# Latent attention with a new opening, split projections and rotations in steps

## The chip, the cores and the metric

The kernel runs on one core of a Trainium2 chip. The metric is the device time of one execution in microseconds (us); smaller is better. The core's engines each work through a queue of their own, in its order: TensorE (PE; its weight loads are shown as PEld), VectorE (DVE), ScalarE (ACT), GpSimd (POOL) and SyncE (SP), which issues most DMAs; ACT's queue issues some. An instruction whose input is not there holds up everything behind it on its engine.

## The reference

Three transformer layers run on 512 positions of width 1024. Only the first layer's mixer and one vector of the last layer matter here. The first mixer is a latent attention with 16 heads:

```python
h = x @ w_in                                   # 512 (c_q) + 256 (c_kv) + 32 (k_rope) columns
q  = (rms_norm(c_q, q_norm) @ w_uq)            # per head 64 plain columns + 32 to rotate
kv = (rms_norm(c_kv, kv_norm) @ w_ukv)         # per head 64 key columns + 64 value columns
q = [q_nope, apply_rope(q_rope)];  k = [k_nope, apply_rope(k_rope)]   # k_rope shared by all heads
out = causal softmax(q k^T / sqrt(96)) @ v;    return out @ w_o
```

In the last layer, `c_act = silu(c)` (1024 numbers) is multiplied with a large matrix to give shifts and scales. All inputs are float32.

## The kernel before

**Precision.** Each operand of a product is split into a high part, rounded by a cast, and a low part, the rest. A product is three matmuls (`mm3`): high by high, and twice high by low. So each weight block ("unit") is loaded as `raw` by SP, cast to `wh` on ACT (L121), and subtracted to `wl` on `lo_eng` (L122): DVE, but POOL inside the attention loop. Activations are split the same way by `split` (ACT cast L160, DVE subtract L161). PE's three matmuls are lines L153 to L155.

**Units.** `use()` hands out the next unit and first prepares all units up to `ahead` further ones (`ensure`, `_prep`), and loads `dma_ahead` beyond. Units 0 to 7 are `w_in`, 8 and 9 the query rotation weights, 10 the values of heads 0 to 7 ("v"), 11 the keys of heads 0 to 7 ("k"), 12 the queries of four heads ("q0"), 13 the values of heads 8 to 15 ("v1"), 14 the next queries ("q1"), 15 further keys ("k1"), 16 and 17 further queries. From 18 on come units of the cross-attention, used as fillers (`FILL_A`).

**Opening.** `front` transposes tiles of 128 positions of x (`tr`, L509) and multiplies them with `w_in`: tiles 0 and 1 together, then 2, then 3. `norm` forms the squared sums on ACT, a chain of small DVE steps (L537 to L184) for the reciprocal root, and `cn` (L542). `back` transposes `cn` (L553) and splits it into `cq` and `ckv`. `trig` makes cosines and sines. Then come the rotated query parts `rq`, in two halves of 256 positions; the second half needs tile 3.

**Attention.** In turn h the kernel runs: the output of head h-3 (`o`), the transposes of head h-2 (`t`, split to `pt`), the normalisation of head h-1 (DVE RECIPROCAL L700, then four products on POOL, L703), the scores of head h (`s`, L689; a DVE pass with the mask L692, then four exponentials on ACT L694), the routine `ahead(h)`, and fillers. `ahead(h)` of an even h projects keys (6 matmuls) and queries (12 matmuls) of the next pair of heads (`proj`, `qk`), and in turns 0, 4 and 8 runs a rotation (`rope`: a DVE shuffle L385, two products L386 and L387, a sum L388, a split) of four heads' queries. `FILL_V` says in which turns blocks of the value projection of heads 8 to 15 run: {1: (0,), 3: (1,), 4: (2, 3)}.

**Order.** The code is not the order. A scheduler of the framework moves each engine's instructions forward as its own model of the time allows; what stands in an engine's queue is fixed at build time. Loads leave SP in the order written: x tiles 0 and 1 with the eight `w_in` units, then eight small tables (`setup`), then x tiles 2 and 3, then the units for q, k and v. The vector `c` is loaded by ACT's queue at the start (`cc`) and used some 400 us later, in `mod_start`, by one ACTIVATE (`cact`, L1003).

Of the kernel before, what the change touches and what calls it, by code (L numbers as in the profile page):

```python
# [9 lines left out]
F = mybir.dt.float32  # L10
# [4 lines left out]
OP = mybir.AluOpType  # L15
# [17 lines left out]

FILL_A = {8: 1, 10: 2, 11: 2, 12: 1, 15: 1, 16: 2, 17: 3}
FILL_B = {2: 1, 3: 1, 4: 1, 6: 1, 9: 1, 11: 1, 12: 1, 14: 1, 17: 1, 19: 1, 20: 1, 22: 1, 24: 1, 27: 1, 28: 1}
FILL_V = {1: (0,), 3: (1,), 4: (2, 3)}
FILL_P = {7: (0,), 8: (1,), 9: (2,), 10: (3,)}
C_ID = 0
C_MASK = 128
# [25 lines left out]
class K:  # L65
# [311 lines left out]
        v.tensor_scalar(cos, cos, -2.0, 1.0, op0=OP.mult, op1=OP.add)  # L377
        self.cos, self.sin = cos, sin

    def rope(self, src, out, eng):  # L380

        nc = self.nc
        t = self.pg(F, "rp")
        t1, t2 = t[:, 0:512], t[:, 512:1024]
        nc.vector.stream_shuffle(t2, src, [(i + 16) % 32 for i in range(32)])  # L385
        eng.tensor_tensor(t1, src, self.cos, op=OP.mult)  # L386
        eng.tensor_tensor(t2, t2, self.sin, op=OP.mult)  # L387
        nc.vector.tensor_tensor(t1, t1, t2, op=OP.add)  # L388
        self.split(out[:, 0], out[:, 1], t1)
# [92 lines left out]
    def mla(self):  # L482
        nc, a = self.nc, self.a
        xd = a["x"][0].rearrange("(t p) d -> p t d", p=128)
        xs = []
        for t in range(NT):
            x = self.pg(F, "x0")
            if t == 0:
                nc.scalar.dma_start(x[:, 512:1024], xd[:, t, 512:1024])
                nc.sync.dma_start(x[:, 0:512], xd[:, t, 0:512])  # L490
            else:
                last = nc.sync.dma_start(x, xd[:, t, :])
            xs.append(x)
            self.load(1 if t == 0 else 8)
            if t == 1:
                self.setup(last)
        us = []
        cq = [[self.pg(R, "cq").rearrange("p (f c) -> p f c", f=2) for _ in range(2)] for _ in range(2)]
        ckv = [self.pg(R, "ckv").rearrange("p (f c) -> p f c", f=2) for _ in range(2)]
        cqs = [[cq[k // 2][h][:, k % 2] for h in range(2)] for k in range(4)]  # L500
        ckvs = [[ckv[h][:, k] for h in range(2)] for k in range(2)]
        krf = self.pg(F, "krf")[:, 0:512]

        def tr(t):
            xT = [self.pg(R, "x0T").rearrange("p (f c) -> p f c", f=8) for _ in range(2)]
# [9 lines left out]
        x0T = {}  # L515

        def front(ts, then=None):
            xT = [x0T.pop(t) if t in x0T else tr(t) for t in ts]
            pp = [(self.ps("pa"), self.ps("pb")) for _ in ts]
            for k in range(8):  # L520
                if len(us) == k:
                    us.append(self.use(3))
                u = us[k]
                for x, (pa, pb) in zip(xT, pp):
                    l = [x[0][:, k], x[1][:, k]]
                    self.mm3(pa, l, [u[0][:, 0:512], u[1][:, 0:512]], k == 0, k == 7)
                    self.mm3(pb[:, 0:288], l, [u[0][:, 512:800], u[1][:, 512:800]], k == 0, k == 7)
                if k == 4 and then is not None:
# [20 lines left out]
        def back(t, scr):  # L549
            c = slice(t * 128, t * 128 + 128)  # L550
            p = self.ps("tp")
            for f in range(4):
                nc.tensor.transpose(p[:, f * 128:(f + 1) * 128], scr[:, f * 128:(f + 1) * 128], self.ident)  # L553
            q = self.ps("tp")
            for f in range(3):
                nc.tensor.transpose(q[:, f * 128:(f + 1) * 128], scr[:, 512 + f * 128:512 + (f + 1) * 128], self.ident)
            p = p.rearrange("p (f c) -> p f c", f=4)
            for i in range(2):
                self.split(cq[i][0][:, :, c], cq[i][1][:, :, c], p[:, 2 * i:2 * i + 2])
            self.split(ckv[0][:, :, c], ckv[1][:, :, c], q[:, 0:256].rearrange("p (f c) -> p f c", f=2))  # L560
            nc.scalar.copy(krf[:, t * 128:(t + 1) * 128], q[:, 256:384])
# [6 lines left out]
        scr.append(norm(2, *pp[2]))  # L568
        self.trig()
        pp += front((3,))  # L570
        back(2, scr[2])
        prev = norm(3, *pp[3])
        self.ahead, self.dma_ahead = 2, 2
        QF = [[self.pair("qf") for _ in range(2)] for _ in range(2)]
        KF = [[self.pair("kf") for _ in range(2)] for _ in range(2)]
        for i in range(2):
            nc.gpsimd.memset(QF[i][1][0:32].bitcast(F), 0.0)
            nc.gpsimd.memset(KF[i][1][0:32].bitcast(F), 0.0)
        ropeq, rps = [], []
        uu = [self.use(), self.use()]  # L580
        for m in range(4):
            rps.append(self.ps("rq"))
        for g in range(2):
            if g == 1:
                back(3, prev)
            for m in range(4):
                for k in range(4):
                    cc = (m % 2) * 128
                    self.mm3(rps[m][:, g * 256:(g + 1) * 256],
                             [uu[m // 2][0][:, k, cc:cc + 128], uu[m // 2][1][:, k, cc:cc + 128]],  # L590
                             [x[:, g * 256:(g + 1) * 256] for x in cqs[k]], k == 0, k == 3)
            if g == 0:
                st = {n: self.use() for n in ("v", "k", "q")}
        V = {}

        def vproj(h, js=range(NT)):
            if h == 1 and js[0] == 0:
                st["v"] = self.use()
            u = st["v"]
            for j in js:  # L600
                p = self.ps("v")
                c = slice(j * 128, j * 128 + 128)
                for k in range(2):
                    self.mm3(p, [x[:, c] for x in ckvs[k]], [u[0][:, k], u[1][:, k]], k == 0, k == 1)
                V[h, j] = self.pair("v")
                self.split(V[h, j][:, 0], V[h, j][:, 1], p)

        kr = self.pair("kr")
        self.rope(krf, kr, nc.vector)
        rsb = [self.pg(F, "rsb") for _ in range(2)]  # L610
        rsb = [rsb[m // 2][:, (m % 2) * 512:(m % 2) * 512 + 512] for m in range(4)]

        def ropes(m):
            rq = self.pair("rq")
            self.rope(rsb[m], rq, nc.vector if m == 0 else nc.gpsimd)
            ropeq.append(rq)
        nc.scalar.copy(rsb[0], rps[0])
        ropes(0)
        for m in range(1, 4):
            nc.scalar.copy(rsb[m], rps[m])  # L620
        for i in range(2):
            nc.scalar.dma_start(KF[i][0][64:96].bitcast(F), kr[64:96].bitcast(F))
            nc.scalar.dma_start(KF[i][1][32:64].bitcast(F), kr[32:64].bitcast(F))
        OT = []
        vproj(0)

        def proj(p):
            if p == 4:
                st["k"] = self.use()
            if p in (2, 4, 6):  # L630
                st["q"] = self.use()
            ring = p % 2
            for hd in range(2):
                h = 2 * p + hd
                rows = slice(64, 96) if hd == 0 else slice(32, 64)
                nc.scalar.dma_start(QF[ring][hd][rows].bitcast(F), ropeq[h // 4][32 * (h % 4):32 * (h % 4) + 32].bitcast(F))
            for src, nk, w, cc, dst in ((ckvs, 2, st["k"], (p % 4) * 128, KF), (cqs, 4, st["q"], (p % 2) * 128, QF)):
# [360 lines left out]
    def mod_start(self):  # L998
        nc, a, cp = self.nc, self.a, self.cp
        cc = cp.tile([128, 8], F, name="cc")  # L1000
        nc.scalar.dma_start(cc, a["c_2"].rearrange("o (k p) -> p (o k)", p=128))
        self.cact = cp.tile([128, 8], F, name="cact")
        self.after(nc.scalar.activation(self.cact, cc, AF.Silu), self.last_act)  # L1003
        self.onesr = cp.tile([128, 128], R, name="onesr")
        nc.vector.tensor_copy(self.onesr, self.ones1.to_broadcast([128, 128]))
        self.modcol = cp.tile([128, 6, 8], F, name="modcol")
        self.gate = {}
        self.mstep, self.mw, self.macc, self.mlimit, self.mpend = 0, {}, {}, 16, None
# [694 lines left out]
```

## Time and profile before

| | us |
|---|---|
| three runs | 2175.51, 2175.67, 2180.46 (median 2175.67) |
| profiled execution, its own time | 2170.42 |
| its span, first to last instruction | 2168.6 |
| PE busy | 2125.2 (98%) |
| DVE / ACT / POOL busy | 1324.1 / 925.7 / 287.9 |
| mean granted TensorE clock | 0.995 of full |

Busy shares alone say that PE bounds the kernel. The changed code covers the first 245 us (the latent attention up to its output projection) and one place near 410 us.

### The profile page before, as it was taken

The page shows a single profiled execution, that of the slowest core. Times are in us where ns is not written, and L with a number is a line of the kernel's source. Part 1 is how long each engine was busy: PE and PEld are TensorE (multiplying, and loading weights), DVE is VectorE, ACT ScalarE, POOL GpSimd, SP SyncE. Part 2 cuts the span into 40 slices and gives each one's busy share as a digit, 9 for nine tenths or more (in the row PEclk, how much of TensorE's full clock was granted, in tenths as well). Part 3 has the DMA queues.
Part 4 walks back from the last instruction along what each step waited for, and adds up shares of the span by engine and source line. Part 5 has one row for each costly group of instructions (what it writes and reads, how often), then busy time and mean ns, then how long its engine had stood idle before and what let it go on. Part 6 is the DMA issues. An engine that isn't in the chain of part 4 may idle for free.

```text
span 2168.6 us, 30013 instructions
## 1 busy us (share of the span) xinstructions
PE 2125.2 (98%) x11492; PEld 1776.7 (82%) x11492; DVE 1324.1 (61%) x2747; ACT 925.7 (43%) x1684; POOL 287.9 (13%) x288
## 2 busy tenths in 40 slices
PE   8999999999999999899999999999999999999998
PEld 7789898988888887775688888888888879888886
DVE  6776566735237267877676845446377677755734
ACT  3687444313225143578734332224224655343521
POOL 0255100000000002476300000000004310000002
PEclk9999999999999999999999999999999999999999
DMA  6123613355324132240332345444320335432311
GB/s 209 49 67 99 205 59 117 96 167 155 97 94 151 54 107 65 77 123 27 125 119 79 117 155 184 136 127 159 104 59 21 88 112 156 146 94 91 126 59 39
DMA packets 254178, 233.82 MB, mean 108 GB/s; under 512 B 14516, under 2 KB 219700, under 8 KB 254036
## 3 DMA queue, kind: packets, MB, share of 16 engines
q1 hardware_dynamic: 246384, 214.19, 32.1%
q10 hardware_dynamic: 7652, 17.73, 2.6%
q8 instruction: 90, 1.47, 0.3%
q14 instruction: 52, 0.43, 0.1%
HBM read 220.81 MB, written 6.82 MB: 105 GB/s over the span
## 4 chain that ended last, share of the span: by engine, by line
PE 53%; DVE 4%; ACT 2%; issue 1%; POOL 0%; DMA 0%; DVEq 0%; ACTq 0%; POOLq 0%
PE fm L154 9%; PE fm L155 9%; PE fm L153 9%; PE acc L153 6%; PE acc L154 6%; PE acc L155 6%; PE s L1252 1%; PE o L153 1%; PE o L154 1%; PE o L155 1%; DVE sc L1172 1%; PE t L1275 1%; PE v L153 1%; DVE qb L1222 1%; DVE m L1169 1%
## 5 line engine op out<-in xcount | busy, mean ns | idle before, releaser
L154 PE MATMUL fm<-xT,wh 128*128 128x512 f32 (+3 forms) x1640 | 588.8, 361 | 0.4
L155 PE MATMUL fm<-xT,wl 128*128 128x512 f32 (+3 forms) x1640 | 588.3, 359 | 0.0
L153 PE MATMUL fm<-xT,wh 128*128 128x512 f32 (+3 forms) x1640 | 587.7, 360 | 0.5 <-ACT wh L121 0.4
L122 DVE TENSOR_TENSOR wl<-raw,wh 128x1024 fp32r<-128x1024 f32 (+1 forms) x299 | 358.3, 1223 | 94.5 <-ACT wh L121 64.4
L121 ACT CAST wh<-raw 128x1024 fp32r<-128x1024 f32 (+2 forms) x339 | 338.9, 1038 | 71.8 <-PE acc L154 18.8
L154 PEld LDWEIGHTS fm<-xT,wh 128*128 128x128 f32 (+2 forms) x1640 | 307.2, 187 | 48.4 <-DVE xT L250 1.6
L155 PEld LDWEIGHTS fm<-xT,wl 128*128 128x128 f32 (+2 forms) x1640 | 307.4, 187 | 47.2 <-DVE wl L122 0.3
L153 PEld LDWEIGHTS fm<-xT,wh 128*128 128x128 f32 (+2 forms) x1640 | 306.4, 187 | 48.2 <-ACT wh L121 0.9
L122 POOL TENSOR_TENSOR wl<-raw,wh 128x1024 fp32r<-128x1024 f32 (+1 forms) x40 | 93.4, 2344 | 1211.3 <-ACT wh L121 610.6
L153 PE MATMUL acc<-wh,hs 128*128 128x512 f32 x528 | 205.6, 389 | 0.0
L154 PE MATMUL acc<-wl,hs 128*128 128x512 f32 x528 | 205.4, 389 | 0.0
L155 PE MATMUL acc<-wh,hs 128*128 128x512 f32 x528 | 204.9, 389 | 0.0
L974 DVE TENSOR_TENSOR hT<-sil,fm 128x512 f32<-128x512 f32 x44 | 30.3, 688 | 228.5 <-PE fm L155 225.7
L973 ACT ACTIVATE sil<-fm 128x512 f32<-128x512 f32 x44 | 26.3, 598 | 300.6 <-PE fm L155 283.5
L153 PEld LDWEIGHTS acc<-wh,hs 128*128 128x128 f32 x528 | 99.1, 188 | 20.5
L957 DVE SCALAR_TENSOR_TENSOR cv<-fm,cw,cv 128x511 f32<-128x511 f32 x88 | 65.8, 748 | 82.2 <-ACT cv L955 81.0
L154 PEld LDWEIGHTS acc<-wl,hs 128*128 128x128 f32 x528 | 99.1, 188 | 20.5
L155 PEld LDWEIGHTS acc<-wh,hs 128*128 128x128 f32 x528 | 99.1, 188 | 20.5
L153 PE MATMUL acc<-wh,ot 128*128 128x512 f32 x288 | 112.5, 391 | 0.0
L155 PE MATMUL acc<-wh,ot 128*128 128x512 f32 x288 | 112.1, 389 | 0.0
L154 PE MATMUL acc<-wl,ot 128*128 128x512 f32 x288 | 112.1, 389 | 0.0
L217 ACT ACTIVATE x<-x,mv 128x1024 f32<-128x1024 f32 x20 | 24.9, 1243 | 147.9 <-DVE mv L216 147.8
(363 smaller groups left out, 3518.7 us busy)
## 6 DMA issues: line engine op xcount, KB each, us to landing
raw<-in_ffn_w_in_dram SPq DMA_DIRECT2D x88, 512.0 KB
mw<-in_mod_w_dram SPq DMA_DIRECT2D x48, 512.0 KB
raw<-in_ffn_w_down_dram SPq DMA_DIRECT2D x44, 512.0 KB
raw<-in_ffn_up_dram SPq DMA_DIRECT2D x44, 512.0 KB
raw<-in_xa_w_kv_dram SPq DMA_DIRECT2D x32, 512.0 KB
raw<-in_ffn_down_dram SPq DMA_DIRECT2D x22, 512.0 KB
raw<-in_xa_w_q_dram SPq DMA_DIRECT2D x16, 512.0 KB
raw<-in_xa_w_o_dram SPq DMA_DIRECT2D x16, 512.0 KB
```

Of the source, the lines that this page charges most:

```text
L121: self.nc.scalar.copy(hi[:, :n], raw[:, :n])
L122: self.lo_eng.tensor_tensor(lo[:, :n], raw[:, :n], hi[:, :n].bitcast(F), op=OP.subtract)
L153: mm(out, l[0], r[0], start=first, stop=False, **kw)
L154: mm(out, l[0], r[1], start=False, stop=False, **kw)
L155: mm(out, l[1], r[0], start=False, stop=last, **kw)
L217: ops.append(lambda: nc.scalar.activation(x, x, AF.Identity, bias=mv[:, 3:4], scale=mv[:, 2:3]))
L957: nc.vector.scalar_tensor_tensor(y[:, sh:], p[:, :S - sh], w[:, 2 - sh, c:c + 1], y[:, sh:], op0=OP.mult, op1=OP.add)
L973: nc.scalar.activation(s, g, AF.Silu)
L974: nc.vector.tensor_tensor(hT[j // 2][:, j % 2], s, u, op=OP.mult)
L1169: m = v.max(m8, sc[b])
L1172: v.match_replace(sc[b], m8, sc[b], -3.0e38)
L1222: ops.append(lambda o=o, i=i: v.tensor_copy(o, i))
```

## The change

- **Loads.** x tiles 2 and 3 are issued before the small tables of `setup`.
- **Front.** The first weight unit is taken after the first tile's transposes, ahead of the second's; the first four products run as block 0 and 1 of tile 0, then of tile 1.
- **Units.** `ahead` is 0 with `dma_ahead` 2 for the units 8 to 13, all taken before or just after the norm of tile 3; then `ahead` is 2. Unit 13 is taken there too. After it nothing is prepared further until q1 is taken, inside turn 3; q1, k1 and q2 are then prepared at once.
- **Values.** Two blocks of v (12 matmuls) run ahead of `back(3)`, two blocks of v1 after `proj(0)`; `FILL_V` keeps the other two.
- **Rotations** are cut into steps. That of the shared key and the first of the queries run interleaved on DVE; the later three follow the table `ROPE` (turn: which rotation, how many steps). The key rows of the first pair are copied sooner, those of the second pair after `proj(0)`.
- **Projections** of a pair: keys in the even turn, queries in the odd one.
- **c** is loaded by ACT's queue after `last_act`, the ACTIVATE `x` (L217) of the last tile, just ahead of its use.

No instruction kind is added or dropped; one `wl` subtraction goes from DVE to POOL.

```diff
-FILL_V = {1: (0,), 3: (1,), 4: (2, 3)}
+FILL_V = {3: (2,), 4: (3,)}
+ROPE = {0: ((1, 2),), 1: ((1, 2),), 3: ((2, 2),), 4: ((2, 1),), 5: ((2, 1),), 7: ((3, 2),), 8: ((3, 1),), 9: ((3, 1),)}
...
-            if t == 1:
-                self.setup(last)
+        self.setup(last)
...
-            xT = [x0T.pop(t) if t in x0T else tr(t) for t in ts]
+            xT = []
+            for t in ts:
+                xT.append(x0T.pop(t) if t in x0T else tr(t))
+                if not us:
+                    us.append(self.use(0))
...
+            if len(ts) == 2:
+                order[:4] = [(0, 0), (1, 0), (0, 1), (1, 1)]
...
+        self.ahead, self.dma_ahead = 0, 2
+        uu = [self.use(), self.use()]
+        st = {"v": self.use()}
         back(2, scr[2])
         prev = norm(3, *pp[3])
-        self.ahead, self.dma_ahead = 2, 2
+        for n in ("k", "q", "v1"):
+            st[n] = self.use()
+        self.ahead = 2
...
             if g == 1:
+                vproj(0, (0, 1))
                 back(3, prev)
...
-            if g == 0:
-                st = {n: self.use() for n in ("v", "k", "q")}
...
+        ks, qs = self.rope_steps(krf, kr, nc.vector), self.rope_steps(rsb[0], ropeq[0], nc.vector)
+        for x, n in ((ks, 1), (qs, 1), (ks, 2), (qs, 1), (ks, 1), (qs, 2)):
+            for _ in range(n):
+                x.pop(0)()
+        krows(0)
...
-        vproj(0)
+        vproj(0, (2, 3))
...
-            if h in (0, 4, 8):
-                ropes(h // 4 + 1)
-            if h % 2 == 0 and h < 14:
-                proj(h // 2 + 1)
+            for m, n in ROPE.get(h, ()):
+                ropes(m, n)
+            if h < 14:
+                proj(h // 2 + 1, (h % 2,))
         proj(0)
+        krows(1)
+        vproj(1, (0, 1))
...
-        nc.scalar.dma_start(cc, a["c_2"].rearrange("o (k p) -> p (o k)", p=128))
+        self.after(nc.scalar.dma_start(cc, a["c_2"].rearrange("o (k p) -> p (o k)", p=128)), self.last_act)
```

PE's queue from the scores of head 3 on, before (`s` scores, `v` value projection, `qk` key or query projection; the numbers tell buffers apart):

```order
L689 MATMUL s_1080<-kf_596,qf_592 128x512 x3
L689 MATMUL s_1078<-kf_596,qf_592 128x384 x3
L689 MATMUL s_1078<-kf_596,qf_592 128x128 x3
L689 MATMUL s_1079<-kf_596,qf_592 128x256 x3
L153 MATMUL v_1104<-wh_663,ckv_114 128x512
L154 MATMUL v_1104<-wl_664,ckv_114 128x512
```

and in the changed kernel:

```order
L713 MATMUL s_1055<-kf_612,qf_608 128x512 x3
L713 MATMUL s_1053<-kf_612,qf_608 128x384 x3
L713 MATMUL s_1053<-kf_612,qf_608 128x128 x3
L713 MATMUL s_1054<-kf_612,qf_608 128x256 x3
L155 MATMUL qk_1102<-cq_110,wh_1084 128x512
L156 MATMUL qk_1102<-cq_111,wh_1084 128x512
L157 MATMUL qk_1102<-cq_110,wl_1085 128x512
```

Behind the scores of head 3 there were value matmuls; now there are the query matmuls with the unit q1 (`wh_1084`, `wl_1085`).

POOL's queue in the same turn, before (`P`, `p` probabilities of a head, `rp` a rotation):

```order
L703 TENSOR_TENSOR P_1081<-P_1081,st_1083 128x512
L703 TENSOR_TENSOR P_1081<-P_1081,st_1083 128x384
L703 TENSOR_TENSOR P_1081<-P_1081,st_1083 128x128
L703 TENSOR_TENSOR p_1082<-p_1082,st_1083 128x256
L386 TENSOR_TENSOR rp_1183<-rsb_748,trig_487 128x512
L387 TENSOR_TENSOR rp_1183<-rp_1183,trig_487 128x512
L703 TENSOR_TENSOR P_1159<-P_1159,st_1161 128x512
```

and in the changed kernel, where `P_1056` and `p_1057` are head 3's:

```order
L389 TENSOR_TENSOR rp_1080<-rsb_755,trig_487 128x512
L390 TENSOR_TENSOR rp_1080<-rp_1080,trig_487 128x512
L727 TENSOR_TENSOR P_1056<-P_1056,st_1058 128x512
L727 TENSOR_TENSOR P_1056<-P_1056,st_1058 128x384
L727 TENSOR_TENSOR P_1056<-P_1056,st_1058 128x128
L124 TENSOR_TENSOR wl_1085<-raw_597,wh_1084 128x1024
L727 TENSOR_TENSOR p_1057<-p_1057,st_1058 128x256
L124 TENSOR_TENSOR wl_1091<-raw_603,wh_1090 128x1024
L124 TENSOR_TENSOR wl_1097<-raw_1088,wh_1096 128x1024
```

Three subtractions of weights (q1, k1, q2) now follow head 3's normalisation; `wl_1085`, the first, stands behind three of its four products.

DVE's queue in the same turn of the changed kernel (`st_1058` is head 3's sums; ISA is the pass with the mask):

```order
L716 ISA p_1057,st_1058<-s_1054,cst 128x256
L716 ISA st_1058 128x1
L391 STREAM_SHUFFLE rp_1080<-rsb_755 128x512
L392 TENSOR_TENSOR rp_1080<-rp_1080 128x512
L724 RECIPROCAL st_1058<-st_1058 128x4
L163 TENSOR_TENSOR qf_605<-qk_1102,qf_605 64x512
L163 TENSOR_TENSOR qf_606<-qk_1102,qf_606 64x512
```

A shuffle and a sum of the rotation, which takes POOL's `rp_1080` products, stand ahead of head 3's reciprocal.

DVE's queue in the norm of tile 3, before (`rs`, `ss` its small steps):

```order
L182 TENSOR_TENSOR rs_572<-ss_568 128x2
L183 TENSOR_TENSOR rs_572<-rs_572 128x2
L184 SCALAR_TENSOR_TENSOR ss_568<-rs_572,ss_568 128x2
L542 SCALAR_TENSOR_TENSOR cn_567<-pa_501,ss_568,nrows_95 128x512
L543 SCALAR_TENSOR_TENSOR cn_567<-pb_502,ss_568,nrows_95 128x256
L545 COPY cn_567<-pb_502 128x128
L122 TENSOR_TENSOR wl_602<-raw_271,wh_601 128x1024
L161 TENSOR_TENSOR cq_111<-tp_675,cq_110 128x2x128
L122 TENSOR_TENSOR wl_658<-raw_289,wh_657 128x1024
```

and in the changed kernel:

```order
L184 TENSOR_TENSOR rs_572<-ss_568 128x2
L185 TENSOR_TENSOR rs_572<-rs_572 128x2
L124 TENSOR_TENSOR wl_590<-raw_271,wh_589 128x1024
L186 SCALAR_TENSOR_TENSOR ss_568<-rs_572,ss_568 128x2
L124 TENSOR_TENSOR wl_594<-raw_289,wh_593 128x1024
L184 TENSOR_TENSOR rs_572<-ss_568 128x2
L124 TENSOR_TENSOR wl_600<-raw_307,wh_599 128x1024
L185 TENSOR_TENSOR rs_572<-rs_572 128x2
L186 SCALAR_TENSOR_TENSOR ss_568<-rs_572,ss_568 128x2
L184 TENSOR_TENSOR rs_572<-ss_568 128x2
```

The subtractions of the units k, q0 and v1, which followed `cn`, now stand between the small steps ahead of it.

## Rows read from the trace of the kernel before

**Rows 1.** By stretch: us, busy per engine (instructions), PEclk, DMA share, GB/s

```profile
0.00:45.00 45.00, 37.85 (x202) 32.71 (x203) 24.78 (x61) 19.62 (x37) 4.29 (x9) 1.00 0.66 216
45.00:81.00 36.00, 31.39 (x191) 28.02 (x189) 29.38 (x72) 16.29 (x36) 1.29 (x1) 0.95 0.28 84
81.00:131.00 50.00, 49.11 (x273) 41.38 (x274) 39.86 (x108) 39.22 (x94) 26.45 (x30) 0.97 0.21 54
```

**Rows 2.** Waits of PE, 0 to 245 us; awaited work, us in total, times, longest

```profile
PE tp L553 <- DVE cn L542: 3.0, 1, 3.0
PE o L153 <- ACT pt L160: 1.7, 2, 1.3
PE s L689 <- ACT qf L160: 1.7, 1, 1.7
...
PE o L154 <- DVE pt L161: 1.1, 2, 0.6
```

**Rows 3.** Waits of the SP queue, 0 to 30 us; same columns

```profile
SPq L113 <- DMA cc<-in_c_dram: 6.9, 1, 6.9
```

**Rows 4.** Timeline of PE, opening; start, us, operation, [idle before <- releaser]

```profile
7.42 1.97 PE L509 MATMUL tp<-cst,x 128*128 128x128 f32 x8 [0.19 <-DMA x<-in_x_dram]
10.83 0.79 PE L153 MATMUL pa<-wh,x0T 128*128 128x512 f32 x1 [1.43 <-ACT wh L121]
...
24.34 1.07 PE L509 MATMUL tp<-cst,x 128*128 128x128 f32 x8 [0.53 <-DMA x<-in_x_dram]
```

**Rows 5.** Timeline of ACT, opening

```profile
9.91 5.42 ACT L121 CAST wh<-raw 128x800 fp32r<-128x800 f32 x7
```

**Rows 6.** Timeline of DVE, norm of tile 3

```profile
57.74 0.16 DVE L537 TENSOR_TENSOR ss<-ss,cst 128x2 f32<-128x2 f32 x1
...
60.31 0.75 DVE L542 SCALAR_TENSOR_TENSOR cn<-pa,ss,nrows 128x512 f32<-128x512 f32 x1
...
61.57 1.22 DVE L122 TENSOR_TENSOR wl<-raw,wh 128x1024 fp32r<-128x1024 f32 x1
```

**Rows 7.** Timeline of PE, v projection

```profile
71.98 0.39 PE L155 MATMUL v<-wh,ckv 128*128 128x512 f32 x1
...
74.70 0.39 PE L155 MATMUL v<-wh,ckv 128*128 128x512 f32 x1
```

**Rows 8.** Clock after the wait for tile 3; columns of rows 1

```profile
63.00:66.00 3.00, 3.00 (x12) 2.61 (x11) 2.90 (x5) 1.68 (x4) 0.00 (x0) 0.50 0.00 0
```

**Rows 9.** Timeline of PE, scores of heads 0 and 4

```profile
81.55 2.80 PE L689 MATMUL s<-kf,qf 96*128 96x512 f32 x11 [0.21 <-DVE kf L161]
...
108.74 2.16 PE L689 MATMUL s<-kf,qf 96*128 96x512 f32 x12
```

**Rows 10.** Timeline of DVE, heads 2 and 4

```profile
97.78 0.68 DVE L692 CUSTOM_DVE_ANT_0 P<-s,cst 128x512 f32<-128x512 f32 x1
...
100.83 0.18 DVE L700 RECIPROCAL st<-st 128x4 f32<-128x4 f32 x1 [1.33 <-ACT p L694]
...
112.94 0.68 DVE L692 CUSTOM_DVE_ANT_0 P<-s,cst 128x512 f32<-128x512 f32 x1
...
116.73 0.69 DVE L388 TENSOR_TENSOR rp<-rp 128x512 f32<-128x512 f32 x1 [0.85 <-POOL rp L387]
```

**Rows 11.** Timeline of POOL, heads 0 to 4

```profile
92.00 0.61 POOL L703 TENSOR_TENSOR p<-p,st 128x256 f32<-128x256 f32 x1
...
98.07 2.41 POOL L122 TENSOR_TENSOR wl<-raw,wh 128x1024 fp32r<-128x1024 f32 x1
...
109.75 2.19 POOL L703 TENSOR_TENSOR P<-P,st 128x512 f32<-128x512 f32 x3 [5.84 <-PE s L689]
```

**Rows 12.** Timeline of ACT, after the output projection

```profile
412.07 0.21 ACT L1003 ACTIVATE cact<-cc 128x8 f32<-128x8 f32 x1
...
416.58 1.24 ACT L217 ACTIVATE x<-x,mv 128x1024 f32<-128x1024 f32 x1 [2.41 <-DVE mv L216]
```

**Rows 13.** Timeline of PE there

```profile
420.78 1.91 PE L232 MATMUL tp<-cst,x 128*128 128x128 f32 x16
```

More of the change, by code (lines that the diff above doesn't have):

```diff
@@ L378, in trig, with rope_steps @@
         self.cos, self.sin = cos, sin
-    def rope(self, src, out, eng):
+    def rope_steps(self, src, out, eng):
         nc = self.nc
@@ L384, in rope, with products @@
         t1, t2 = t[:, 0:512], t[:, 512:1024]
[L385 to L389, printed above, removed]
+        def products():
+            eng.tensor_tensor(t1, src, self.cos, op=OP.mult)
+            eng.tensor_tensor(t2, t2, self.sin, op=OP.mult)
+        return [lambda: nc.vector.stream_shuffle(t2, src, [(i + 16) % 32 for i in range(32)]), products,
+                lambda: nc.vector.tensor_tensor(t1, t1, t2, op=OP.add), lambda: self.split(out[:, 0], out[:, 1], t1)]
     def plan(self):
@@ L517, in front @@
         def front(ts, then=None):
-            xT = [x0T.pop(t) if t in x0T else tr(t) for t in ts]
+            xT = []
[3 more added lines that the diff above has]
+                    us.append(self.use(0))
             pp = [(self.ps("pa"), self.ps("pb")) for _ in ts]
-            for k in range(8):
+            order = [(k, i) for k in range(8) for i in range(len(ts))]
+            if len(ts) == 2:
+                order[:4] = [(0, 0), (1, 0), (0, 1), (1, 1)]
+            for k, i in order:
                 if len(us) == k:
                     us.append(self.use(3))
[L523 to L528, printed above, removed]
+                u, x, (pa, pb) = us[k], xT[i], pp[i]
+                l = [x[0][:, k], x[1][:, k]]
+                self.mm3(pa, l, [u[0][:, 0:512], u[1][:, 0:512]], k == 0, k == 7)
+                self.mm3(pb[:, 0:288], l, [u[0][:, 512:800], u[1][:, 512:800]], k == 0, k == 7)
+                if k == 4 and i == len(ts) - 1 and then is not None:
                     x0T[then] = tr(then)
@@ L579, in mla, with vproj @@
         ropeq, rps = [], []
-        uu = [self.use(), self.use()]
         for m in range(4):
             rps.append(self.ps("rq"))
+        V = {}
+        def vproj(h, js=range(NT)):
+            u = st["v1" if h else "v"]
+            for j in js:
+                p = self.ps("v")
+                c = slice(j * 128, j * 128 + 128)
+                for k in range(2):
+                    self.mm3(p, [x[:, c] for x in ckvs[k]], [u[0][:, k], u[1][:, k]], k == 0, k == 1)
+                V[h, j] = self.pair("v")
+                self.split(V[h, j][:, 0], V[h, j][:, 1], p)
         for g in range(2):
             if g == 1:
+                vproj(0, (0, 1))
                 back(3, prev)
@@ L591, in mla @@
                              [x[:, g * 256:(g + 1) * 256] for x in cqs[k]], k == 0, k == 3)
-            if g == 0:
-                st = {n: self.use() for n in ("v", "k", "q")}
[L594 to L606, printed above, removed]
@@ L608, in mla, with ropes @@
         kr = self.pair("kr")
-        self.rope(krf, kr, nc.vector)
         rsb = [self.pg(F, "rsb") for _ in range(2)]
         rsb = [rsb[m // 2][:, (m % 2) * 512:(m % 2) * 512 + 512] for m in range(4)]
[L613 to L616, printed above, removed]
-        nc.scalar.copy(rsb[0], rps[0])
-        ropes(0)
+        steps = {}
+        def ropes(m, n):
+            if m not in steps:
+                ropeq.append(self.pair("rq"))
+                steps[m] = self.rope_steps(rsb[m], ropeq[m], nc.gpsimd)
+            for _ in range(n):
+                steps[m].pop(0)()
@@ new lines, in krows @@
+        def krows(i):
+            nc.scalar.dma_start(KF[i][0][64:96].bitcast(F), kr[64:96].bitcast(F))
+            nc.scalar.dma_start(KF[i][1][32:64].bitcast(F), kr[32:64].bitcast(F))
+        nc.scalar.copy(rsb[0], rps[0])
+        ropeq.append(self.pair("rq"))
+        ks, qs = self.rope_steps(krf, kr, nc.vector), self.rope_steps(rsb[0], ropeq[0], nc.vector)
+        for x, n in ((ks, 1), (qs, 1), (ks, 2), (qs, 1), (ks, 1), (qs, 2)):
+            for _ in range(n):
+                x.pop(0)()
@@ L619, in mla, with proj @@
+        krows(0)
         for m in range(1, 4):
             nc.scalar.copy(rsb[m], rps[m])
-        for i in range(2):
-            nc.scalar.dma_start(KF[i][0][64:96].bitcast(F), kr[64:96].bitcast(F))
-            nc.scalar.dma_start(KF[i][1][32:64].bitcast(F), kr[32:64].bitcast(F))
         OT = []
-        vproj(0)
-        def proj(p):
-            if p == 4:
+        vproj(0, (2, 3))
+        def proj(p, which=(0, 1)):
+            if p == 4 and 0 in which:
                 st["k"] = self.use()
-            if p in (2, 4, 6):
+            if p in (2, 4, 6) and 1 in which:
@@ L631, in proj @@
                 st["q"] = self.use()
             ring = p % 2
-            for hd in range(2):
+            for hd in range(2 if 0 in which else 0):
                 h = 2 * p + hd
@@ L636, in proj @@
                 nc.scalar.dma_start(QF[ring][hd][rows].bitcast(F), ropeq[h // 4][32 * (h % 4):32 * (h % 4) + 32].bitcast(F))
-            for src, nk, w, cc, dst in ((ckvs, 2, st["k"], (p % 4) * 128, KF), (cqs, 4, st["q"], (p % 2) * 128, QF)):
+            for i in which:
+                src, nk, w, cc, dst = ((ckvs, 2, st["k"], (p % 4) * 128, KF), (cqs, 4, st["q"], (p % 2) * 128, QF))[i]
                 q = self.ps("qk")
```

## The prediction

> **What bounds the kernel now.** I first read the stretches of the opening and the attention [rows 1]. PE works 37.85 of the first 45 us, 31.39 of the next 36 and 49.11 of the next 50: 12.7 us of idle in 131 us, and the attention loop, from 81 us, is nearly full. The granted clock is below 1.00 in two stretches: 0.95 of 36 us and 0.97 of 50 us, or 1.8 and 1.5 us lost. In the slice behind the longest hole it is 0.50 [rows 8], the lower of two levels, 1.2 instead of 2.4 GHz; the engine had idled before it. All the change can win there is 12.7 + 3.3 = 16 us. PE's waits name the holes [rows 2]: 3.0 us for tile 3's normalised values, 1.7 for the first queries' split ahead of head 0, 1.7 and 1.1 for `pt` later on. In the opening the first product waits 1.43 for a weight cast and tile 2's transposes 0.53 for x [rows 4]; SP's queue stood 6.9 us for `cc` [rows 3]. These are the places that the change touches. After them I read the order of the changed kernel, and there one new wait is larger than all of these.
>
> **The change part by part.** Terms in us of the profiled execution, plus is slower.
>
> *Opening: −2.0.* The first weight cast starts at 9.91 [rows 5], behind both tiles' casts, and PE's first product at 10.83. With the cast ahead of tile 1's transposes the weight is ready while PE transposes; the product can follow the end of these, 7.42 + 1.97 = 9.39 [rows 4]: −1.43. Tile 2's x is issued ahead of eight small tables, and without the 6.9 us of `cc`: the 0.53 goes. Lower end −0.5, if the weights' DMAs are what is late next; upper end −3, if the waits of PE inside the first products shrink too. I take the middle, as both rows name their releasers.
>
> *Norm of tile 3: +0.5.* From the first small step to `cn` DVE takes 60.31 − 57.74 = 2.57 [rows 6], and PE waits 3.0 for it [rows 2]. Now three weight subtractions of 1.22 stand inside the chain. Each adds its 1.22, less what it covers of the small steps' gaps: some 3.2 in all. In the hole stand 12 value matmuls, whose weights are ready by then; 12 of them lie between 71.98 and 74.70 [rows 7], 2.7. So +0.5 of further idle, with both ends at 0 and +3.2 (the matmuls moved there leave elsewhere).
>
> *Head 0: −1.9 and −1.5.* The 1.66 + 0.21 ahead of its scores [rows 2, 9] gets two blocks of v1; with the hole goes the clock loss of that stretch, 1.5 [rows 1].
>
> *First transposes and head 2: +3.8, and +0.8.* Before, head 0's probabilities were normalised at 92.00 + 0.61 = 92.6 [rows 11], 8.3 after the end of head 0's scores (81.55 + 2.80 = 84.35 [rows 9]). That chain on DVE, ACT and POOL stays. PE's queue between now holds 18 projection matmuls and 12 scores: 18 × 0.227 (2.72 / 12, [rows 7]) + 2.1 [rows 9] = 6.2, since the six value matmuls have left and the clock is full. So 2.1 idle; then head 2's scores wait for the queries' split, which ACT does behind head 1's exponentials, as the same wait did for 1.7 ahead of head 0 [rows 2]. Half a clock loss (0.8) comes with it. Ends: 0 and 5.
>
> *Head 3: +10.8, and +1.7.* Here the main term is. Before, q1's `wl` was made on DVE during the opening, long ahead of its use; now it is made when turn 3 asks for it, and PE reaches its product directly behind head 3's scores. It takes the low weights `wl_1085`, which POOL makes behind three products of head 3's normalisation, which wait for the reciprocal, which DVE runs behind the mask passes, the shuffle and the sum of a rotation. In steps: head 4 of the trace has the same DVE work; its passes start at 112.94, 2.0 after its scores ended at 108.74 + 2.16 [rows 9, 10]. To the end of the rotation's sum it is 116.73 + 0.69 − 112.94 = 4.5 [rows 10]. The reciprocal is 0.18 [rows 10], POOL's three products 2.2, its subtraction 2.4 [rows 11]. Sum 2.0 + 4.5 + 0.2 + 2.2 + 2.4 = 11.3, less 0.46 for the two matmuls that need the high part alone: 10.8. Behind the waiting matmul stand head 0's last value blocks, head 1's output, head 2's transposes and head 4's scores, none of which PE can take first; so it is lost whole. After such a hole the clock was lost before; 1.7 is the mean of the two losses, 1.8 and 1.5 [rows 1]. Lower end +7: the passes start with the first finished block of scores (2.0 and some 1.5 less) and no clock loss. Upper end +14.
>
> *Head 11: +2.6.* The same pattern with cross-attention weights, without a rotation: passes 1.9 behind the scores, 100.83 − 97.78 = 3.1 to the reciprocal [rows 10], then 0.2 + 2.2 + 2.4: 9.8. PE has 12 query matmuls (2.7), 24 of 256 columns (2.9) and eight of an output (1.5) ahead: 7.1. Ends 0 and 4.
>
> *Waits for `pt`: −1.4.* Of 1.7 + 1.1 [rows 2] I count half, since projections now stand in odd turns too; ends 0 and −2.8.
>
> *`cc`: +0.5.* `cact` starts at 412.07, 4.5 ahead of the ACTIVATE of x at 416.58 [rows 12], and PE transposes that tile from 420.78 [rows 13], 3.0 after the ACTIVATE's end. Now the load is issued just before `cact`, and ACT stands until it lands. So a load of up to 7.5 costs nothing, and each us beyond it costs one. SP's queue waited 6.9 for this load at the start [rows 3], which is a part of its time, though with the DMAs busy (0.66 of the stretch, [rows 1]). I take 0.5; ends 0 and 5, a load of 12.5.
>
> The Trainium skill, "DMA: Bandwidth & Descriptors", section "Rules for kernel authors", speaks against this edit: issue a DMA early and wait on it late, and a last dimension that isn't contiguous becomes one descriptor per element (as the 1024 numbers of `c` are). By it the load is the late one, and the sum would be 4 higher; the trace's 6.9 us for 4 KB [rows 3] agrees as far as one row goes.
>
> Other edits cost nothing that I can see: rotations are the same instructions, in steps DVE had idle room for.
>
> **Sum:** −2.0 + 0.5 − 1.9 − 1.5 + 3.8 + 0.8 + 12.5 + 2.6 − 1.4 + 0.5 = +13.9; the profiled execution, 2170.42 (its span 2168.6 and 1.8 around it), would become 2184. The median of the three runs lies 5.25 above that execution; on 2175.67, rounding the many small terms down a little, I say 2189.
>
> **The rivals.** (1) *The new wait at head 3 is short.* DVE runs the passes beside the scores and the clock does not fall: +7.3 there, nothing at head 11, no clock loss at head 2: −2.0 + 0.5 − 3.4 + 3.8 + 7.3 − 1.4 + 0.5 = +5.3, or 2181. For it: PE gives its blocks one by one. Against: in the trace passes start 1.9 to 2.0 late each time [rows 9, 10]. (2) *Faster.* One mechanism: with the value work moved ahead PE comes to its queue's later places after the other engines, not before them as I count, so `wl_1085` is there when it reaches `qk_1102`. Then the old holes are filled and no new one takes their place: −(2.0 + 3.0 + 1.9 + 2.8 + 3.3) = −13.0, or 2163. It decides at the end of `wl_1085` against the end of head 3's scores: without head 3's and head 11's waits the sum of my other terms is −1.2, so a wait of more than a microsecond there is a loss. For it: the 12.7 us of idle are there [rows 1]. Against: DVE's and POOL's queues are in order, and the chain starts from these very scores, however late PE comes. (3) *`cc` lands late:* as forecast, +4, or 2193.
>
> **How the numbers follow.** The forecast has 0.66, (1) 0.15, (2) 0.09, (3) 0.10. A difference under 0.3% (6.5 us) can't be told from none here. (2) is faster. Most of (1), at +5.3, lies within 0.3%, and a little of the forecast's lower end (the ends at head 3 and head 2 together take away 8): 0.16 for the same. The rest, 0.75, is slower. The range goes from 2177, just below (1), to 2198, (3) with the upper end of head 3; the forecast's own is 2182 to 2195.
>
> **What would show it.** In the changed kernel's waits of PE the largest is `qk` for `wl`, made on POOL, about 11 us in one piece near 105 us, with the granted clock below 1.00 behind it; a smaller one for head 11. The first product starts near 9.4, `cc` no longer holds SP, and the wait for `cn` is near 3.5 with matmuls in front of it. I am wrong if `wl_1085` ends before head 3's scores do, or if PE's sum of idle in the first 131 us falls below 12.7.

## The result and the profile after

The changed kernel takes 2190.03 us (median of four runs, 2188.98 to 2191.54) against 2175.59 before: the ratio is 1.0065, with a 95% interval of 1.0051 to 1.0078, or 11 to 17 us slower. The forecast was 2189. Its profiled execution took 2190.53 (span 2188.7, mean clock 0.989).

PE's waits from 0 to 245 us (awaited work, total, times, longest), to be held against [rows 2]:

```profile
PE tp L561 <- DVE cn L550: 5.0, 1, 5.0
PE qk L155 <- ACT wh L123: 4.6, 1, 4.6
...
PE qk L157 <- POOL wl L124: 4.0, 1, 4.0
PE k L157 <- POOL wl L124: 2.6, 1, 2.6
PE t L735 <- POOL p L727: 1.9, 2, 1.6
PE t L735 <- POOL P L727: 1.4, 2, 1.0
...
PE s L713 <- ACT qf L162: 0.6, 1, 0.6
```

The small waits of before for the first queries, and for `pt`, are gone or smaller. In their place stand 4.6 and 4.0 us at one product, `qk`, at first for the cast of q1 on ACT, then for its subtraction on POOL; 2.6 for a weight of the cross-attention (head 11); 3.3 for the probabilities of head 0 and of a later head; and the wait for tile 3's `cn` has grown from 3.0 to 5.0.

The stretches of [rows 1], in the changed kernel:

```profile
0.00:45.00 45.00, 39.19 (x216) 34.20 (x217) 26.53 (x66) 20.06 (x40) 2.88 (x8) 1.00 0.66 234
45.00:81.00 36.00, 31.02 (x182) 27.93 (x181) 27.84 (x67) 15.09 (x30) 3.30 (x3) 0.91 0.09 23
81.00:131.00 50.00, 38.90 (x179) 30.54 (x178) 29.00 (x78) 29.24 (x71) 22.28 (x23) 0.80 0.20 53
```

The reader is to see that two columns fell. PE works 38.90 of the 50 us from 81 to 131 instead of 49.11, and there the granted clock is 0.80 instead of 0.97. Idle in the first 131 us is 21.9 us instead of 12.7. The clock alone accounts for 10 us in the last of these rows; a part of that lies inside the waits, where it costs nothing.

**Where the time went.** I set the starts of the same instructions in both traces against each other, and count a matmul that one kernel has done earlier than the other at 0.227 us.

| up to | before | after | extra work done by then | lag | step |
|---|---|---|---|---|---|
| end of tile 3's products (start of the last) | 51.44 | 48.90 | | −2.5 | −2.5 |
| first key projection | 74.93 | 75.65 | | +0.7 | +3.2 |
| end of head 0's scores | 84.35 | 84.53 | 12 matmuls | −2.5 | −3.2 |
| end of head 3's scores | 104.76 | 107.79 | 6 fewer | +4.4 | +6.9 |
| start of head 4's scores | 108.74 | 125.61 | 6 more | +15.5 | +11.1 |
| start of the output projection | 244.9 | 262.1 | | +17.2 | +1.7 |

All that the change touches, but for the load of `c`, lies ahead of the last line. The profiled execution lost 2.9 more in the attention of the second layer; the kernel before, run again, took as long there (last run below).

**Head 3**, on PE, DVE, ACT and POOL (start, us, operation), against [rows 9 to 11]. PE:

```profile
105.63 2.16 PE L713 MATMUL s<-kf,qf 128*128 128x512 f32 x12
112.38 0.80 PE L155 MATMUL qk<-cq,wh 128*128 128x512 f32 x1 [4.60 <-ACT wh L123]
112.97 0.63 PE L156 MATMUL qk<-cq,wh 128*128 128x512 f32 x1
117.57 0.79 PE L157 MATMUL qk<-cq,wl 128*128 128x512 f32 x1 [3.97 <-POOL wl L124]
```

DVE:

```profile
108.39 0.68 DVE L716 CUSTOM_DVE_ANT_0 P<-s,cst 128x512 f32<-128x512 f32 x1
...
112.13 0.69 DVE L392 TENSOR_TENSOR rp<-rp 128x512 f32<-128x512 f32 x1 [1.38 <-POOL rp L390]
112.74 0.17 DVE L724 RECIPROCAL st<-st 128x4 f32<-128x4 f32 x1
```

ACT:

```profile
111.30 2.92 ACT L123 CAST wh<-raw 128x1024 fp32r<-128x1024 f32 x3
```

POOL:

```profile
113.04 2.18 POOL L727 TENSOR_TENSOR P<-P,st 128x512 f32<-128x512 f32 x3 [0.95 <-issue]
115.18 2.34 POOL L124 TENSOR_TENSOR wl<-raw,wh 128x1024 fp32r<-128x1024 f32 x1
```

The scores end at 107.79; the mask passes start 0.6 behind them, the rotation's sum ends at 112.82, the reciprocal at 112.91, POOL's three products at 115.22, its subtraction at 117.52, and PE's third matmul starts at 117.57. That is the chain of the prediction, link by link, 9.8 us long with two matmuls inside it. Those two didn't run right behind the scores, though: they need the high weights, and ACT casts these from 111.30 on, behind head 3's exponentials.

### The profile page after: what moved, and what is told of

Same layout as the page of the kernel before. It is cut to its first block, busy times and chain, and to the rows that moved or that the text cites. A ratio compares the mean times of both kernels' runs of the same rounds, so it can differ in the third digit from the quotient of the medians.

```text
span 2188.7 us, 30023 instructions
## 1 busy us (share of the span) xinstructions
PE 2131.8 (97%) x11492; PEld 1780.5 (81%) x11492; DVE 1326.9 (61%) x2746; ACT 924.2 (42%) x1684; POOL 290.2 (13%) x289
## 4 chain that ended last, share of the span: by engine, by line
PE 85%; DVE 5%; ACT 2%; POOL 1%; issue 1%; DMA 1%; SPq 0%; POOLq 0%; DVEq 0%; ACTq 0%
PE fm L156 14%; PE fm L155 14%; PE fm L157 14%; PE acc L155 9%; PE acc L156 9%; PE acc L157 9%; PE v L155 1%; PE o L156 1%; PE o L155 1%; PE o L157 1%; PE s L713 1%; PE v L157 1%; PE v L156 1%; PE t L735 1%; PE s L1276 1%
```

## The experiments

The main theory: the low weights of q1, made late and behind head 3's normalisation, hold PE, and the clock falls with it. The rivals: PE would have waited there anyhow; or the time is lost at the first transposes, or at the norm of tile 3. The start of the output projection (262.1 in the changed kernel, 244.9 before) measures each kernel's first layer in its trace.

**q1 prepared early.**

```diff
         vproj(1, (0, 1))
+        self.ensure(15)
```

> The changed kernel, with the unit q1 prepared (cast on ACT, subtraction on DVE) right behind the first pair's projections, ahead of the loop; k1 and q2 are still prepared in turn 3. Theory (the late low weights of q1 hold PE at head 3): the two waits of 4.6 and 4.0 us and the half clock behind them go, 9.8 + 1.7 = 11.5 us, so the start of the output projection moves from 262.1 to about 250.6 us and the kernel to about 2179, a ratio to before of 1.000 to 1.003. Rival (PE would have waited at head 3 anyhow, for the normalisation or the transposes): under half of that, 2184 or more.

The projection starts at 246.1, 16.0 us earlier; 2181.97 us, 1.0028 of before (1.0015 to 1.0042). The product after head 3's scores runs on without a wait:

```profile
101.83 2.18 PE L714 MATMUL s<-kf,qf 128*128 128x512 f32 x12
103.84 0.40 PE L155 MATMUL qk<-cq,wh 128*128 128x512 f32 x1
...
104.31 0.40 PE L157 MATMUL qk<-cq,wl 128*128 128x512 f32 x1
```

The theory holds, and the saving is larger than the 11.1 of the table's step: one more unit is ready at each later place too, so the 2.6 us of head 11 are gone, and the clock falls for a shorter time behind the first transposes. The end-to-end time shows less of it, 8 us: in that trace the second layer's attention took 178.1 us at a granted clock of 0.93, in the changed kernel's 173.1 at 0.96, and all behind it 2 more.

**The low weights late, but on DVE.**

```diff
             if p in (2, 4, 6) and 1 in which:
+                if p == 2:
+                    self.lo_eng = nc.vector
+                    self.ensure(self.cur + 1)
+                    self.lo_eng = nc.gpsimd
                 st["q"] = self.use()
```

> The changed kernel, with the low weights of q1 alone made on DVE, still in turn 3 when they are asked for: on DVE they stand right behind head 3's reciprocal, on POOL nothing else moves. Theory (the chain mask pass, rotation's sum, reciprocal, then POOL's three products and subtraction): the ACT wait of 4.6 us stays, the wait for the low weights falls from 4.0 to about 0.6 (ready near 114.1 instead of 117.5), and the output projection starts some 3.5 us earlier than 262.1. Rival (what holds PE is ACT's cast, with the rest beside it): no change.

PE there:

```profile
111.55 0.80 PE L155 MATMUL qk<-cq,wh 128*128 128x512 f32 x1 [4.58 <-ACT wh L123]
...
113.25 0.79 PE L157 MATMUL qk<-cq,wl 128*128 128x512 f32 x1 [0.47 <-DVE wl L124]
```

The wait for ACT's cast stays, the other falls from 4.0 to 0.5, and the projection starts at 257.7, 4.4 earlier (one execution, 2186.24). So POOL's place behind the normalisation costs some 4 us; with that gone, ACT's cast behind head 3's exponentials still holds PE for 4.6.

**Late units on the kernel before.**

```diff
-        self.ahead, self.dma_ahead = 2, 2
+        self.ahead, self.dma_ahead = 0, 2
...
-                st = {n: self.use() for n in ("v", "k", "q")}
+                st = {n: self.use() for n in ("v", "k", "q", "v1")}
+                self.ahead = 2
```

(`vproj(1)` then uses the unit taken here.)

> The kernel before with one part alone: units 8 to 13 with nothing prepared ahead, v1 taken with k and q0, so that q1, k1 and q2 are first prepared in turn 2, where the projections of that kernel (keys and queries in one turn) ask for q1. Theory (what costs is that the asked-for unit stands on POOL behind the normalisation of the head just scored): here the subtraction stands behind head 1's normalisation, one head earlier, so PE waits only some 3 us at the query product of turn 2, and the output projection starts 3 to 5 us later than 244.9. Rival (late preparation alone costs it all): 10 us or more later.

The projection starts at 245.2, and PE waits 0.3 and 1.2 us:

```profile
96.33 0.50 PE L153 MATMUL qk<-cq,wh 128*128 128x512 f32 x1 [0.27 <-ACT wh L121]
...
98.91 0.51 PE L155 MATMUL qk<-cq,wl 128*128 128x512 f32 x1 [1.15 <-POOL wl L122]
```

Not even the 3 us of the theory. Late preparation alone costs next to nothing where keys and queries share a turn, since the six key matmuls come between and the subtraction stands behind the normalisation of the head before. Of the kernels run, only those with both, late units and queries in the odd turn right behind the scores, have the large wait. Which of the two reasons counts for more was not tried.

**Weights behind the norm.**

```diff
-        for n in ("k", "q", "v1"):
-            st[n] = self.use()
-        self.ahead = 2
...
+        for n in ("k", "q", "v1"):
+            st[n] = self.use()
+        self.ahead = 2
         kr = self.pair("kr")
```

> The changed kernel, with the units k, q0 and v1 taken behind the rotated queries, so that their three subtractions stand behind tile 3's normalised values on DVE, not inside the chain ahead of them. Theory (the subtractions in the chain cost PE 3.5 us and lengthen the half clock there): tile 3's transposes start near 60 us instead of 63.44, PE's wait falls from 5.0 to about 1.5, and the output projection starts 3 to 5 us earlier, kernel about 2186. Rival (the subtractions now delay the rotations and the first queries as much): 2190.

2182.59, 1.0038 (1.0023 to 1.0054); the projection starts at 254.1, 8.0 earlier, and tile 3's transposes at 57.90, 5.5 earlier, with no wait left. That is more than the three subtractions can account for. The changed kernel's DVE in the norm of tile 3:

```profile
57.02 0.16 DVE L545 TENSOR_TENSOR ss<-ss,cst 128x2 f32<-128x2 f32 x1
...
58.11 1.23 DVE L124 TENSOR_TENSOR wl<-raw,wh 128x1024 fp32r<-128x1024 f32 x1
...
59.32 1.22 DVE L124 TENSOR_TENSOR wl<-raw,wh 128x1024 fp32r<-128x1024 f32 x1
...
60.53 1.22 DVE L124 TENSOR_TENSOR wl<-raw,wh 128x1024 fp32r<-128x1024 f32 x1
...
62.64 0.75 DVE L550 SCALAR_TENSOR_TENSOR cn<-pa,ss,nrows 128x512 f32<-128x512 f32 x1
```

From the first small step to `cn` it takes 5.62 instead of the 2.57 of [rows 6]: 3.05 more, near the 3.2 of the prediction. But the chain starts only 0.7 us earlier than before, not 2.5, and the reason stands one tile earlier. DVE in the norm of tile 2 (0.16 or 0.17 us each before), and POOL at that time:

```profile
42.96 0.16 DVE L545 TENSOR_TENSOR ss<-ss,cst 128x2 f32<-128x2 f32 x1 [0.62 <-ACT cn L544]
43.16 0.55 DVE L176 TENSOR_SCALAR rs<-ss 128x2 f32<-128x2 f32 x1
43.74 0.92 DVE L177 TENSOR_SCALAR rs<-rs 128x2 int32<-128x2 int32 x1
43.82 0.85 DVE L179 TENSOR_SCALAR rs<-rs 128x2 f32<-128x2 f32 x1
44.70 0.89 DVE L178 TENSOR_SCALAR ss<-rs 128x2 int32<-128x2 int32 x1
45.62 0.16 DVE L184 TENSOR_TENSOR rs<-ss 128x2 f32<-128x2 f32 x1
...
47.38 0.75 DVE L550 SCALAR_TENSOR_TENSOR cn<-pa,ss,nrows 128x512 f32<-128x512 f32 x1
```

```profile
42.73 0.95 POOL L590 MEMSET qf<- 32x1024 f32 x1 [41.59 <-PE pb L157]
43.69 0.94 POOL L591 MEMSET kf<- 32x1024 f32 x1
44.58 0.98 POOL L590 MEMSET qf<- 32x1024 f32 x1
45.50 0.97 POOL L591 MEMSET kf<- 32x1024 f32 x1
```

Four small steps take 0.55 to 0.92 us, each until one of POOL's memsets of the padding rows ends. In this run the memsets run from 35 to 41 us, and the same steps take 0.17:

```profile
42.30 0.16 DVE L545 TENSOR_TENSOR ss<-ss,cst 128x2 f32<-128x2 f32 x1 [0.63 <-ACT cn L544]
42.49 0.17 DVE L176 TENSOR_SCALAR rs<-ss 128x2 f32<-128x2 f32 x1
...
44.87 0.75 DVE L550 SCALAR_TENSOR_TENSOR cn<-pa,ss,nrows 128x512 f32<-128x512 f32 x1
```

So tile 2's chain takes 4.42 us in the changed kernel and 2.57 in this run: 1.85 more, which is what tile 3's chain is late by (2.5 less 0.7).

The memsets were not moved by a line of the diff; they follow, in the code, the units that were taken ahead of them. All traces with the memsets in that place (the changed kernel, q1 early, q1 on DVE, values in turns) have the four long steps, those with them elsewhere don't. No run moved the memsets alone.

**The opening alone, on the kernel before** (loads, front and `c` as in the change).

> The kernel before with the opening alone: x tiles 2 and 3 ahead of the small tables, the first weight cast between the tiles' transposes, the new order of the first four products, c loaded late. Theory (the opening's gain is lost at the norm of tile 3, which on DVE waits behind the cosines, not for PE): tile 3's last product ends 2.5 us earlier, but tile 3's transposes start only about 0.7 earlier, and the kernel gains 0.7 us or nothing that can be measured. Rival (the gain is kept): -2.5 us.

2171.21, 0.9985 (0.9973 to 0.9997). The projection starts at 242.3, 2.6 earlier; tile 3's transposes start at 58.04 instead of 61.21. My theory falls: DVE's chain came forward with PE, and the gain is kept. In the changed kernel the 1.85 us beside the memsets take most of it.

**Early value blocks back in their turns.**

```diff
-        vproj(1, (0, 1))
...
-FILL_V = {3: (2,), 4: (3,)}
+FILL_V = {1: (0,), 3: (1, 2), 4: (3,)}
```

> The changed kernel, with the two early blocks of v1 moved from ahead of head 0's scores back into turns 1 and 3, as before; all else as changed. Theory (moving them away left PE without work ahead of the first transposes, and the clock fell for 10 us): the 1.65 us of idle before the transposes and the 0.9 before head 2's scores and the half clock from 93 to 104 us (5.1 lost) go, and the wait of 1.9 ahead of head 0's scores, with a clock loss of 1.5, comes back: about -4, or 2186. Rival (the hole at the transposes is set by the chain on DVE, ACT and POOL, and returns as it was): 2190.

2192.86, 1.0082 (1.0065 to 1.0099); the projection starts at 261.6. No gain: a wait of 1.2 ahead of head 0's scores returns, the clock doesn't fall behind the transposes, but PE then comes sooner to head 3 and waits 6.3 + 3.9 there instead of 4.6 + 4.0. Whatever is won ahead of head 3 is partly paid back there, since DVE and ACT set when q1 is ready.

**Both mended**, the edits of the first and fourth run together.

> The changed kernel with both edits at once: q1 prepared ahead of the loop, and the units k, q0 and v1 taken behind the rotated queries. Theory (two separate causes, each with a trace of its own): their savings at the start of the output projection, 16.0 and 8.0 us from 262.1, add up to 238, 7 us earlier than in the kernel before (244.9), and the kernel gains about 5 to 7 us on it, 2169 to 2171. Rival (one hole serves both: PE that comes earlier to the loop waits there for DVE, ACT and POOL): 242 to 246, no gain on the kernel before, 2173 to 2176.

2176.99, 1.0006 (0.9995 to 1.0016). The projection starts at 240.9, 4.0 ahead of before; the two savings don't add up to 24 but to 21.2, so the rival is half right. PE's remaining hole is ahead of the first transposes:

```profile
86.42 0.33 PE L736 MATMUL t<-cst,P 128*128 128x128 f32 x1 [2.78 <-POOL P L728]
87.20 0.76 PE L736 MATMUL t<-cst,P 128*128 128x128 f32 x3 [0.46 <-POOL P L728]
```

End to end nothing can be told from the kernel before.

**Three units early**, `self.ensure(17)` in place of 15.

> As the run with both edits, with k1 and q2 prepared ahead of the loop as well, on DVE: POOL is rid of two subtractions of 2.4 us in turn 3, DVE has two of 1.2 more ahead of head 0. Theory: POOL isn't late in turn 3 any more once q1 is early, so nothing is gained, and DVE's 2.4 us ahead of head 0's passes cost 0 to 2.4. Rival (POOL's later normalisations are what the loop waits for): -2.

2177.41, 1.0012 (1.0003 to 1.0021); 243.2 in its trace, 2.3 behind the run above: as the theory had it.

**One value block moved.** On top of both edits `vproj(1, (0,))` ahead of the loop and `FILL_V` = {1: (1,), 3: (2,), 4: (3,)}.

> As the run with both edits, with one of the two early blocks of v1 in turn 1, ahead of the first transposes, instead of ahead of head 0's scores. Theory (PE's remaining hole is ahead of the first transposes, 2.8 + 0.5 us with a clock loss of 1.7 behind it, since that time is set by head 0's chain on DVE, ACT and POOL and PE has no work there): 6 matmuls, 1.4 us, fall into the hole, and head 0's chain starts 1.4 earlier, so the output projection starts 1.4 to 3 us ahead of 240.9. Rival (the hole opens ahead of head 0's scores instead): 240.9 or later.

2175.21, 0.9998 (0.9987 to 1.0008); 241.6. The rival: the hole ahead of the transposes shrinks to 1.4 us, one of 1.1 opens ahead of head 0's scores.

**The second rotation**, on top of it: whole in turn 1, and whole ahead of the loop.

> As the run before it in this list, with the whole second rotation in turn 1 (before: shuffle and products in turn 0, sum and split in turn 1), so that its sum no longer stands on DVE ahead of head 0's reciprocal. Theory (head 0's chain sets PE's hole): a further 1 us or less ahead, since the shuffle still stands there. Rival: the queries of heads 4 and 5, which take the rotation's rows, come late, 2 us back.

> The same with the whole second rotation ahead of the loop: its shuffle, sum and split stand on DVE ahead of head 0's mask passes and its products on POOL as before. Theory: head 0's passes start some 1 to 2 us later (the sum waits for POOL's products, 2.6), but nothing of the rotation is left inside the chain, so the output projection starts within 1.5 us of the run in turn 1. Rival (everything on DVE ahead of head 0 delays the loop one for one): 2 to 3 us later.

In turn 1: 2172.44, 0.9992 (0.9981 to 1.0003), 242.5 in its trace, 0.9 behind the run above instead of up to 1 ahead. Ahead of the loop: one execution, 2167.51, with 241.9, as the theory had it. The first time is within the noise; the second's lower time comes from the second layer, 170.5 us for its attention. So no version here is shown to beat the kernel before but the opening alone, by 0.15%.

One thing stays open. The median time less the start of the projection in the trace is 1934 to 1936 us for four kernels with q1 early (q1 early, both mended, three units early, one value block moved). It is 1928 to 1931 for all others with four or more executions, the rotation in turn 1 among them, which has q1 early too. So some 8 of the 16 us that early q1 wins in the first layer do not show end to end. The time goes with the mean granted clock: the twelve executions of both mended run from 2168.72 us at 0.993 to 2180.98 at 0.988. What lowers the clock there no run shows.

**The kernel before again.**

> The kernel before, unchanged, for a second trace. The changed kernel's trace lost 17.2 us up to the output projection of the first layer and 2.9 more inside the attention of the second layer (from its first score, 890.9 to 1061.0 before, 908.0 to 1081.1 after), which the change doesn't touch. Theory (that stretch varies from execution to execution with the clock, and the first trace of before was a short one): the stretch takes 172 to 176 us here instead of 170.1, while the output projection starts within 0.5 us of 244.9. Rival (the change reaches there): 170 again.

The score products of the second layer's attention (last column but the shapes: first and last start), changed kernel and this run:

```profile
L1271 PE MATMUL s<-kt,qb x64: 192/375/497, 908.0 to 1081.1; 128*128 128x64 f32 x8, 128*128 128x128 f32 x8, 128*128 128x192 f32 x8, 128*128 128x256 f32 x8
```

```profile
L1247 PE MATMUL s<-kt,qb x64: 192/377/497, 892.1 to 1065.3; 128*128 128x64 f32 x8, 128*128 128x128 f32 x8, 128*128 128x192 f32 x8, 128*128 128x256 f32 x8
```

173.1 and 173.2 us, both at a granted clock of 0.96; the first trace of before had 170.1 at 0.97, and the other traces here have 170.5 to 178.1. So the 2.9 us there are not shown to be an effect of the change, and one trace's end-to-end time says less than its first 250 us. The projection started at 246.2, not 244.9: head 0's scores waited 2.96 for the DMA of the rotated rows (`qf<-rq`) in this execution, 1.3 more than [rows 2] had. The change's cost in the first layer is thus 16 to 17 us.

## Why the prediction was right, step by step

The time (2189 for 2190.03) and the main mechanism were right: PE stands behind head 3's scores, and POOL's subtraction ends the wait. That the time fits to a microsecond is in part luck. The sum was +13.9, the traces give 16 to 17 for the first layer, and the medians differ by 14.4. Two terms were too small by 2.7 and 2.3, others too large. By its own terms:

- *Opening, −2.0:* −2.5. The first product starts at 9.56, tile 2's wait for x is gone. PE's first transposes wait 1.15 for x instead, and the products follow:

```profile
6.71 3.20 PE L511 MATMUL tp<-cst,x 128*128 128x128 f32 x12 [1.15 <-DMA x<-in_x_dram]
9.56 0.78 PE L155 MATMUL pa<-wh,x0T 128*128 128x512 f32 x1
```

- *Norm of tile 3, +0.5:* +3.2, the worst-sized term. The 3.2 of subtractions were right (3.05), and the 12 value matmuls stand in the hole. Missing were the 1.85 us that tile 2's chain lost beside the memsets, which nothing in the prediction looked for, and 1.4 more of lost clock (0.91 of 36 us instead of 0.95).
- *Head 0, −3.4:* −3.2.
- *First transposes and head 2, +4.6:* +6.9. The holes are 2.5 us, less than the 3.8; the clock behind them cost more than the 0.8 I counted. It was at half from 93 to 104 us:

```profile
93.00:96.00 3.00, 2.20 (x8) 1.47 (x8) 2.30 (x4) 2.96 (x9) 1.83 (x3) 0.58 0.59 206
96.00:99.00 3.00, 2.67 (x9) 2.20 (x9) 2.94 (x6) 0.93 (x2) 1.55 (x3) 0.50 0.37 83
99.00:102.00 3.00, 3.00 (x9) 2.42 (x10) 1.68 (x10) 2.29 (x8) 0.00 (x0) 0.50 0.05 10
102.00:105.00 3.00, 3.00 (x17) 2.10 (x16) 0.85 (x2) 0.78 (x2) 2.69 (x4) 0.72 0.00 0
```

- *Head 3, +12.5:* +11.1. The passes followed the scores by 0.6 and not 2.0 us; the other links were right within 0.1. The loss of clock was 1.6 us (ten matmuls from 117.57 to 121.46, 3.9 instead of 2.3); 1.7 had been taken. What the prediction had wrong here is the high weights: it took them as ready, and let two matmuls run at once. They came only at 112.38 from ACT. POOL's chain ends later and hid this in the sum, but it shows with q1 late on DVE: without POOL's part 4.6 us of wait stay.
- *Head 11 and `pt`, +1.2:* +1.7; head 11's wait is 2.6, as forecast.
- *`cc`, +0.5:* 0. ACT's rows there:

```profile
426.36 0.39 ACTq L1025 DMA_DIRECT2D cc<-in_c_dram  x1
...
432.64 0.21 ACT L1027 ACTIVATE cact<-cc 128x8 f32<-128x8 f32 x1 [1.54 <-DMA cc<-in_c_dram]
433.81 1.25 ACT L219 ACTIVATE x<-x,mv 128x1024 f32<-128x1024 f32 x1 [0.96 <-DVE mv L218]
```

The load took at most 6.3 us from its issue, ACT stood for 1.54 of it, and the next ACTIVATE of x waited for DVE, not for ACT. PE transposes that tile from 437.95, 17.2 later than in [rows 13], the lag that it had at the output projection: it saw nothing.

Rival (1) let the passes begin some 1.5 us before the scores end, the forecast 2.0 behind; 0.6 behind lies between them, and the clock fell, against (1); (2) needed `wl_1085` before the end of head 3's scores, and it came 9.7 after; (3) did not happen. The profile's signs: about 11 us in one piece near 105 us was 4.6 + 4.0 with two matmuls between at 107.8 to 117.6; the wait for `cn` is 5.0, not 3.5, and so the largest in one piece.

## What to carry to other kernels

Where weights are prepared on demand by in-order engines, look in each engine's queue at what stands ahead of the preparation: a product placed right behind the work that feeds that queue waited for the whole chain here, and a request in the turn before (with six key matmuls between, and behind the earlier head's normalisation) cost 1.4 us of waits instead of 8.6. Idle that was filled at one place was in part paid again at the next wait that another engine set; measure the stretch up to a fixed instruction, since the rest of the kernel may vary by more than the edit. And a line that isn't in the diff can move: the memsets did, because code ahead of them grew.

## What the hardware showed that was not expected

- DVE's small steps on 128x2 elements with a scalar (TENSOR_SCALAR) took 0.55 to 0.92 us instead of 0.17 while POOL ran a memset; each ended with the memset, at 43.7, 44.6 and 45.6 us. The steps with two tensors ran at their 0.16 beside the last memset (45.62 and on). The Trainium skill ("GPSIMD Engine Reference", "Key points") says that POOL shares its SBUF interfaces with VectorE and that they contend with DVE instructions in a 2-port mode or with two SBUF inputs. The first kind may be what is seen here, but no row tells in which mode the steps ran; for the two-tensor steps, beside a MEMSET whose row names no input, this trace shows no delay.
- The clock's fall behind a hole of the same kind differed between traces: behind the first transposes 5.1 us were lost in the changed kernel (the four slices above), in the run with q1 early 1.7 (0.61 and 0.82 in two slices of 3 us).
- ACT's load of 1024 single numbers, 4 KB, was there at most 6.3 us after its issue (426.36 to 432.64), with the DMA engines at 0.97 busy from 424 to 434 us; at the start, with the same load in flight, SP's queue had stood 6.9 [rows 3].
